# Split sums of squares and low parts on VectorE in a hybrid decoder layer

## The chip, the cores and the metric

The kernel runs on one core of one Trainium2 chip. The metric is the device time of one execution in microseconds (us): the median of the runs shown. A profile was taken of one execution.

The engines carry these names in the views: PE is TensorE's matmul and PEld its weight load, DVE is VectorE, ACT is ScalarE, POOL is GpSimd, and SP is SyncE, which here only issues DMAs. Each engine works through its own queue in order.

## The reference

One layer of a decoder is computed for a prompt of 2048 positions and 8 single-position samples, with a model width of 1024, 12 heads of 64 in three groups and a feed-forward width of 4096, all in float32:

```
shift1,scale1,g1,shift2,scale2,g2 = silu(c) @ w_ada + b_ada
h  = RMSNorm(x)*(1+scale1)+shift1
[u | q | k | v | a_pool | a_attn] = h @ w_in
x += g1 * ( sig(a_pool)*(PoolMix(u) @ w_pool_br) + sig(a_attn)*(DilatedAttn(q,k,v) @ w_attn_br) ) @ w_out
h2 = RMSNorm(x)*(1+scale2)+shift2
x += g2 * relu(h2 @ w_up)^2 @ w_down
```

PoolMix takes trailing means over 2, 4, 8 and 16 positions. DilatedAttn attends, in the three head groups, to 128 earlier positions at distances 1, 4 and 16. Before that each head of q and k is divided by the root mean square of its 64 elements and rotated (rope). The rotated keys and the values of the windows are returned too.

## The kernel before

**Number format.** Every large product is made of three products at TensorE's single rate in the type float32r: an operand is split into a high part (a cast to float32r on ACT) and a low part (the operand minus its high part), and high x high, high x low and low x high are summed. `mm3` issues them (24 products for one output tile of the width 1024). A product of plain float32 operands, as `small` issues it, is also used for small things, the sums of squares among them.

**Stages.** The positions are worked on in two phases (`ci` 0: the first 1024 positions and the 8 samples, `ci` 1: the other 1024), each in column groups of 512, 256 and 264 (phase 0) or 512 and 512 (phase 1). In order: the opening (`opening`: the first modulation blocks, the first norm and the first products); q, k and v of phase 0 (`qkv`), by head groups 2, 1, 0; gates, the rest of the modulation and the samples' attention; the pool branch of phase 0 and then of phase 1; q, k and v of phase 1 with the prompt's attention between its products; more gates; and from about 1375 us on, for each phase, the output projection (`project`), the second norm (`norm2`) and the feed-forward part (`up`, `down`), which fills the span from about 1530 us to the end.

**What sets the order.** TensorE's instructions run in the order in which the program writes them. The class `Order` keeps a planned time: each product adds its nominal nanoseconds, and generators that were spawned go on when the planned time has passed the amount that they yielded. The other engines' queues, SP's among them, are ordered by a scheduler when the kernel is built; `first()` gives the instructions in it a higher priority there. At run time every queue is in order, and an instruction that waits holds up those behind it.

**Weights.** `weights` (L213) hands out weights in the order of a plan and issues the load of the next one ahead. `load_w` (L178) loads 512 KB into one of three raw buffers, casts the high part on ACT (L183) and makes the low part on the engine that it was given (L184). `weights` always gives it POOL; the modulation weights `w_ada` use VectorE. A raw buffer can be loaded again when its low part is done.

**Modulated rows.** `modulated` (L317) is called by `make_h` (L356) for the first norm and by `norm2` (L1246) for the second, for each of the eight blocks k of 128 channels: a multiply on VectorE (L320), scale and shift on ACT (L321), high part on ACT (L326), low part on VectorE for even k and on POOL for odd k (L327).

**q and k.** For each of the 30 column groups of a q or k tile pair, `qk_out` (L388) evacuates two tiles on ACT, as values (`ab`, L390) and as squares (`qsq`, L391), and `after_qk` (L400) is spawned: it loads the rope table (L404, SP), adds the squares of the two halves on POOL (L405), makes the two sine products on POOL (L409, L411), the cosine products and sums on VectorE (L410, L412 to L414), and waits in the plan for `HS_AT` = 6500 ns. Then one float32 product with the matrix `hones` (1 where two rows belong to the same head) sums the squares per head and spreads the sum (L417), the root is taken on ACT (L419) and the reciprocal on VectorE (L420), both halves are scaled (L422), cast on ACT (L444), their low parts made on POOL (L445), and the four pieces are stored by SP (L450, L453, L456). The tile for these pieces (`ohl`) has one buffer; the table (`cs`) has two in phase 0 and one in phase 1. `hones` is a part of the packed constants, loaded first of all.

Of the kernel before, what the change touches and what calls it, by code (L numbers as in the profile page):

```python
# [16 lines left out]
P = 128  # L17
# [11 lines left out]
DEPTH = 1  # L29
HS_AT = 6500  # L30
ADA_GAP = 3600
# [20 lines left out]
PRIO = 400  # L52
CPACK = (("cT", (8, 9)), ("bada", (48,)), ("gn", (2, 8)), ("ident", (128,)), ("ones", (128,)), ("hones", (128,)),
         ("mask", (256,)), ("qkg", (2, 2)), ("psc", (4,)), ("icnt", (4, 16)), ("stT", (4, 8, 15)), ("fold", (9,)),
# [60 lines left out]
def emit(tc, I, O):  # L115
# [33 lines left out]
    def first():  # L149
        return tc.high_priority(offset=PRIO)  # L150
# [17 lines left out]
    def small(ps, w, x, ns=220.0):  # L168
        mm(ps, w, x, True, True, ns)
# [40 lines left out]
    issued = [0]  # L210
    depth = [DEPTH]

    def weights(*key):  # L213

        i = issued[0] - len(ready)
        assert plan[i] == key, (plan[i], key)
        while issued[0] < len(plan) and issued[0] <= i + depth[0]:
            k = plan[issued[0]]
            src = I[k[0]][k[1]] if len(k) == 2 else I[k[0]][k[1], :, k[2] * 1024:(k[2] + 1) * 1024]
            ready.append(load_w(src, G, *(extra if issued[0] == 3 else ())))  # L220
            issued[0] += 1
        return ready.pop(0)
# [4 lines left out]
    cv = {}  # L227
    off = 0
    for name, shape in CPACK:
# [7 lines left out]
        off += n  # L237
    cT, ident, ones, hones, mask = cv["cT"], cv["ident"], cv["ones"], cv["hones"], cv["mask"]
    bada, gn, qkg, icnt, stT = cv["bada"], cv["gn"], cv["qkg"], cv["icnt"], cv["stT"]
    epsc = cst.tile([P, 1], F32, name="epsc")  # L240
    V.memset(epsc, EPS)
# [74 lines left out]

    def modulated(hf, x, xr, rs, n, i, k, dst, c0, samp, eng):  # L317

        sh = (0 if i == 0 else 24) + k
        V.tensor_tensor(out=xr, in0=x, in1=rs[:, :n], op=ALU.mult)  # L320
        S.activation(out=hf[:, :n], in_=xr, func=AF.Identity, scale=sc[:, i, k, 0:1], bias=mod[:, sh, 0:1])  # L321
        if samp:
            sl = slice(n - NS, n)
            V.tensor_tensor(out=hf[:, sl], in0=xr[:, sl], in1=sc[:, i, k, 1:9], op=ALU.mult)
            V.tensor_tensor(out=hf[:, sl], in0=hf[:, sl], in1=mod[:, sh, 1:9], op=ALU.add)
        S.copy(out=dst[:, k, 0, c0:c0 + n], in_=hf[:, :n])  # L326
        eng.tensor_tensor(out=dst[:, k, 1, c0:c0 + n], in0=hf[:, :n], in1=dst[:, k, 0, c0:c0 + n].bitcast(F32), op=ALU.subtract)  # L327

# [9 lines left out]
    def hx(hb, nk, c0, n):  # L338
        return [(hb[:, k, 0, c0:c0 + n], hb[:, k, 1, c0:c0 + n]) for k in range(nk)]
# [16 lines left out]
    def make_h(ci, hi, xs, rs, hb, ks=range(KD)):  # L356
        c0, n, splits = HALVES[ci][hi]
        for k in ks:
            hf = npl.tile([P, 520], F32, tag="sq", bufs=3, name="hf")
            modulated(hf, xs[k], xs[k], rs, n, 0, k, hb, c0, ci == 0 and hi == 1, G if k % 2 else V)  # L360

# [31 lines left out]
    def qkv(ci, hb, done=None):  # L393
# [6 lines left out]
        def after_qk(g, qk, t0, n, ab, sq):  # L400
# [3 lines left out]
            SP.dma_start(out=cs[:, :, :n], in_=I["rope"][:, :, BASE[ci] - 1024 * ci + t0:BASE[ci] - 1024 * ci + t0 + n])  # L404
            G.tensor_tensor(out=sq[:, 0, :n], in0=sq[:, 0, :n], in1=sq[:, 1, :n], op=ALU.add)  # L405
            a, b, co, si = ab[:, 0, :n], ab[:, 1, :n], cs[:, 0, :n], cs[:, 1, :n]
            t = ap.tile([P, 2, 512], F32, tag="rt", bufs=1, name="rt")
            o = ap.tile([P, 2, 512], F32, tag="ro", bufs=2, name="ro")
            G.tensor_tensor(out=t[:, 0, :n], in0=b, in1=si, op=ALU.mult)  # L409
            V.tensor_tensor(out=o[:, 0, :n], in0=a, in1=co, op=ALU.mult)  # L410
            G.tensor_tensor(out=t[:, 1, :n], in0=a, in1=si, op=ALU.mult)  # L411
            V.tensor_tensor(out=o[:, 1, :n], in0=b, in1=co, op=ALU.mult)  # L412
# [3 lines left out]
            pst = stp.tile([P, 512], F32, tag="st", name="ps_hs")  # L416
            small(pst[:, :n], hones, sq[:, 0, :n], n / 0.6)  # L417
            rs = ap.tile([P, 512], F32, tag="qrs", bufs=2 - ci, name="qrs")
            S.activation(out=rs[:, :n], in_=pst[:, :n], func=AF.Sqrt, scale=1.0 / 64, bias=epsc)  # L419
            V.reciprocal(out=rs[:, :n], in_=rs[:, :n])  # L420
            for i in range(2):
                V.tensor_tensor(out=o[:, i, :n], in0=o[:, i, :n], in1=rs[:, :n], op=ALU.mult)  # L422
            ohl = ap.tile([P, 2048], F32R, tag="ohl", bufs=1, name="ohl")
            dst = (kst if qk else qst)[g]
# [323 lines left out]
    def opening():  # L748
# [10 lines left out]
        x1 = load_x0(op, 1)  # L759
        raws[3] = ada_load(op, 3)  # L760
        hxs = hx(h0, KD, 0, 512)

# [483 lines left out]
    def norm2(ci, hi, acc, hb, xa):  # L1246
        c0, n, splits = HALVES[ci][hi]
        yield 2500
        rs = rms_finish(tp, stp, acc, splits)
        for k in range(KD):  # L1250
            hg, hf = wtile("hg"), wtile("hf")
            modulated(hf, xa[k][:, c0:c0 + n], hg[:, :n], rs, n, 1, k, hb, 0, ci == 0 and hi == 1, G if k % 2 else V)

# [67 lines left out]
    for ci in range(2):  # L1321
# [15 lines left out]
        br = od.spawn(branches(ci, 1, hbs[1], GAP_B), 3000)  # L1337
        depth[0] = DEPTH_O
        acc = project(ci, 0, hbs[0], xa, load_xa)
        od.drain(br)  # L1340
# [140 lines left out]
```

## Time and profile before

| | |
|---|---|
| runs (us) | 3063.06, 3064.57, 3058.80 |
| median (us) | 3063.06 |
| profiled execution (us) | 3062.32 |
| its span, first to last instruction (us) | 3060.5 |
| mean granted TensorE clock, share of full speed | 0.98 |

The span is what the views divide up; the execution's own time lies 1.8 us above it. A group of instructions is given with its busy time, the mean of one in nanoseconds and the idle time of its engine just before it, with what ended that. A busy TensorE is not one at its peak, since the ends of its products are modelled and overlap.

### The profile page before, as it was taken

The numbers are of one execution on the slowest core, as the hardware profiler recorded it, in microseconds if no ns is written. First come the engines' busy times: TensorE is split into PE (matmuls) and PEld (weight loads), VectorE is DVE, ScalarE is ACT, GpSimd is POOL, SyncE is SP. The second block draws the span as 40 slices with busy tenths as digits, with TensorE's granted clock in tenths as the row PEclk, the third lists the DMA queues.
The fourth block names the chain that finished last, engine by engine and source line by source line (L and its number), as shares of the span: only waits on it lengthen the run. The fifth ranks groups of instructions, "written<-read, shape, count | busy, mean of one in ns | idle before, by whom it ended". The sixth has DMA issues, their size and how long they took to land.

```text
span 3060.5 us, 40917 instructions
## 1 busy us (share of the span) xinstructions
PE 2933.8 (96%) x16220; PEld 2510.3 (82%) x16220; DVE 1590.5 (52%) x2649; ACT 982.3 (32%) x1772; POOL 966.2 (32%) x510
## 2 busy tenths in 40 slices
PE   6899999999898799999999999999999999999999
PEld 3899788887787688878899999999877888888887
DVE  5556442541744534456865545555677554444444
ACT  5333342433554534433521221121235211111211
POOL 2665341433533312233532122122245312221221
PEclk7999999999999889999999999999999999999999
DMA  6544752335777779876321111111272211111111
GB/s 239 172 144 154 270 183 92 118 118 151 200 196 203 186 191 229 239 243 218 105 78 48 43 49 49 42 51 47 92 242 83 76 42 56 48 49 42 55 43 69
DMA packets 207599, 379.09 MB, mean 124 GB/s; under 512 B 47424, under 2 KB 103072, under 8 KB 206624
## 3 DMA queue, kind: packets, MB, share of 16 engines
q1 hardware_dynamic: 195888, 359.63, 38.6%
q10 hardware_dynamic: 11520, 16.85, 1.5%
q8 instruction: 128, 2.10, 0.3%
q14 instruction: 63, 0.52, 0.1%
HBM read 294.89 MB, written 81.75 MB: 123 GB/s over the span
## 4 chain that ended last, share of the span: by engine, by line
PE 76%; DMA 5%; DVE 5%; issue 4%; POOL 3%; ACT 2%; SPq 1%; ACTq 0%; DVEq 0%; POOLq 0%
PE ps_dn L153 23%; PE ps_up L153 22%; PE ps_g L153 10%; PE ps_v L153 4%; PE ps_qk L153 4%; PE ps_wo L153 3%; PE ps_u L153 3%; PE ps_o L153 1%; PE ps_pb L153 1%; POOL wh L184 1%; PE ps_s L153 1%; PE ps_ada L153 1%; DMA slab<-kst 1%; DMA cs<-in_rope 1%; PE ps_ab L153 1%
## 5 line engine op out<-in xcount | busy, mean ns | idle before, releaser
L184 POOL TENSOR_TENSOR wh<-wr,wh 128x1024 fp32r<-128x1024 f32 (+1 forms) x274 | 649.3, 2377 | 1637.9 <-ACT wh L183 1620.7
L153 PE MATMUL ps_dn<-rt,wh 128*128 128x512 f32 (+2 forms) x3840 | 727.0, 350 | 5.3 <-POOL wh L184 3.3
L153 PEld LDWEIGHTS ps_dn<-rt,wh 128*128 128x128 f32 x3840 | 619.6, 188 | 108.2 <-POOL wh L184 4.2
L183 ACT CAST wh<-wr 128x1024 fp32r<-128x1024 f32 (+1 forms) x306 | 309.4, 1023 | 737.9 <-issue 564.0
L1306 DVE SCALAR_TENSOR_TENSOR xa<-ps_dn,mod,xa 128x512 f32<-128x512 f32 (+1 forms) x640 | 405.2, 642 | 202.1 <-PE ps_dn L153 195.9
L153 PE MATMUL ps_g<-h,wh 128*128 128x512 f32 (+2 forms) x1920 | 389.6, 354 | 0.4 <-POOL wh L184 0.4
L153 PE MATMUL ps_up<-hb,wh 128*128 128x264 f32 (+2 forms) x2304 | 371.7, 319 | 0.0
L153 PE MATMUL ps_up<-ha,wh 128*128 128x512 f32 x1536 | 367.3, 395 | 0.0
L153 PEld LDWEIGHTS ps_up<-hb,wh 128*128 128x128 f32 x2304 | 332.3, 188 | 36.1
L153 PEld LDWEIGHTS ps_g<-h,wh 128*128 128x128 f32 x1920 | 307.2, 190 | 48.5 <-POOL wh L184 1.0
L153 PEld LDWEIGHTS ps_up<-ha,wh 128*128 128x128 f32 x1536 | 286.6, 188 | 66.3 <-issue 0.5
L153 PE MATMUL ps_qk<-h,wh 128*128 128x512 f32 (+2 forms) x1440 | 301.4, 362 | 14.2 <-POOL wh L184 4.9
L1290 DVE TENSOR_TENSOR r<-r 128x512 f32<-128x512 f32 (+2 forms) x160 | 99.3, 621 | 389.2 <-ACT r L1289 389.1
L153 PEld LDWEIGHTS ps_qk<-h,wh 128*128 128x128 f32 x1440 | 233.6, 193 | 58.5 <-POOL h L327 6.3
L1292 DVE TENSOR_TENSOR rt<-r,rt 128x512 fp32r<-128x512 f32 (+2 forms) x160 | 218.0, 1362 | 81.7 <-ACT rt L1291 81.6
L1289 ACT ACTIVATE r<-ps_up 128x512 f32<-128x512 f32 (+2 forms) x160 | 82.1, 513 | 416.8 <-PE ps_up L153 416.8
L153 PE MATMUL ps_v<-wh,h 128*128 128x256 f32 (+1 forms) x1224 | 171.6, 297 | 25.4 <-ACT wh L183 19.3
L153 PEld LDWEIGHTS ps_v<-wh,h 128*128 128x128 f32 (+1 forms) x1224 | 157.8, 195 | 30.5 <-ACT wh L183 19.7
L945 ACT ACTIVATE pe<-pe,ost 128x128 f32<-128x128 f32 (+1 forms) x192 | 87.1, 454 | 142.5 <-DVE ost L943 139.5
L943 DVE CUSTOM_DVE_ANT_0 pe<-ps_s,cp 128x128 f32<-128x128 f32 (+1 forms) x192 | 61.5, 358 | 118.2 <-PE ps_s L153 118.0
L1291 ACT CAST rt<-r 128x512 fp32r<-128x512 f32 (+2 forms) x160 | 85.7, 536 | 66.4 <-DVE r L1290 66.4
L445 POOL TENSOR_TENSOR ohl<-ro,ohl 128x256 fp32r<-128x256 f32 (+1 forms) x66 | 76.1, 1175 | 92.4 <-ACT ohl L444 81.8
(182 smaller groups left out, 2981.7 us busy)
## 6 DMA issues: line engine op xcount, KB each, us to landing
wr<-in_w_up SPq DMA_DIRECT2D x72, 512.0 KB
wr<-in_w_down SPq DMA_DIRECT2D x68, 512.0 KB
wr<-in_w_in SPq DMA_DIRECT2D x64, 512.0 KB
wr<-in_w_ada SPq DMA_DIRECT2D x48, 512.0 KB
slab<-kst SPq DMA_DIRECT2D x40, 512.0 KB
wr<-in_w_out SPq DMA_DIRECT2D x32, 512.0 KB
cs<-in_rope SPq DMA_DIRECT2D x18, 512.0 KB
qst<-ohl SPq DMA_DIRECT2D x9, 1024.0 KB
```

The source lines that it names most:

```text
L153: PE.matmul(ps, w, x, start=start, stop=stop)
L183: S.copy(out=wt[:, 0, :n], in_=raw[:, :n])
L184: eng.tensor_tensor(out=wt[:, 1, :n], in0=raw[:, :n], in1=wt[:, 0, :n].bitcast(F32), op=ALU.subtract)
L445: G.tensor_tensor(out=pl, in0=pi, in1=ph.bitcast(F32), op=ALU.subtract)
L943: V.tensor_tensor_reduce(out=pe[:, off:off + nk], in0=ps[:, off:off + nk], in1=mask[:, mo:mo + nk], scale=-0.125, scalar=3.0e38, op0=ALU.a ...
L945: S.activation(out=pe[:, off:off + nk], in_=pe[:, off:off + nk], func=AF.Exp, scale=-1.0, bias=o[:, 64:65], accum_out=o[:, 65:66])
L1289: S.activation(out=r1[:, :l], in_=ps[:, :l], func=AF.Relu)
L1290: V.tensor_tensor(out=r1[:, :l], in0=r1[:, :l], in1=r1[:, :l], op=ALU.mult)
L1291: S.copy(out=rt[:, 0, a:a + l], in_=r1[:, :l])
L1292: V.tensor_tensor(out=rt[:, 1, a:a + l], in0=r1[:, :l], in1=rt[:, 0, a:a + l].bitcast(F32), op=ALU.subtract)
L1306: V.scalar_tensor_tensor(out=x[:, c0 + a:c0 + a + lp], in0=ps[:, :lp], scalar=mod[:, 40 + m, 0:1], in1=x[:, c0 + a:c0 + a + lp], op0=ALU.m ...
```

## The change

The low parts of the modulated rows are all made on VectorE. `weights` gives `load_w` the engine `weng[0]`, which is VectorE until the output projection of phase 0 begins and POOL from there on. The two sine products of the rope go to VectorE. The sum of squares per head is split into a high part (ACT) and a low part (VectorE), and two single-rate products with `hones` take the place of the float32 one; they are planned 9000 ns after the column group instead of 6500. The two parts live in the buffers of the gates' tile `th` (two buffers; a group of 512 or 264 columns takes both, one of 256 takes one). `hones` becomes a float32r constant of its own, loaded in the opening through a raw weight buffer and cast on ACT. `ohl` has two buffers in phase 0.

```diff
-HS_AT = 6500
+HS_AT = 9000
...
-CPACK = (("cT", (8, 9)), ("bada", (48,)), ("gn", (2, 8)), ("ident", (128,)), ("ones", (128,)), ("hones", (128,)),
+CPACK = (("cT", (8, 9)), ("bada", (48,)), ("gn", (2, 8)), ("ident", (128,)), ("ones", (128,)), 
...
+    weng = [V]
...
-            ready.append(load_w(src, G, *(extra if issued[0] == 3 else ())))
+            ready.append(load_w(src, weng[0], *(extra if issued[0] == 3 else ())))
...
+    hones = cst.tile([P, P], F32R, name="hones")
...
-    def modulated(hf, x, xr, rs, n, i, k, dst, c0, samp, eng):
+    def modulated(hf, x, xr, rs, n, i, k, dst, c0, samp):
...
-        eng.tensor_tensor(out=dst[:, k, 1, c0:c0 + n], in0=hf[:, :n], in1=dst[:, k, 0, c0:c0 + n].bitcast(F32), op=ALU.subtract)
+        V.tensor_tensor(out=dst[:, k, 1, c0:c0 + n], in0=hf[:, :n], in1=dst[:, k, 0, c0:c0 + n].bitcast(F32), op=ALU.subtract)
...
             G.tensor_tensor(out=sq[:, 0, :n], in0=sq[:, 0, :n], in1=sq[:, 1, :n], op=ALU.add)
+
+            m = 1 if n > 256 else 2
+            hl = [gtp.tile([P, m, 512 // m], F32R, tag="th", bufs=2, name="sqhl") for _ in range(2 // m)]
+            sh, sl = (hl[0][:, 0, :n], hl[-1][:, m - 1, :n])
+            with first():
+                S.copy(out=sh, in_=sq[:, 0, :n])
+                V.tensor_tensor(out=sl, in0=sq[:, 0, :n], in1=sh.bitcast(F32), op=ALU.subtract)
...
-            G.tensor_tensor(out=t[:, 0, :n], in0=b, in1=si, op=ALU.mult)
+            V.tensor_tensor(out=t[:, 0, :n], in0=b, in1=si, op=ALU.mult)
             V.tensor_tensor(out=o[:, 0, :n], in0=a, in1=co, op=ALU.mult)
-            G.tensor_tensor(out=t[:, 1, :n], in0=a, in1=si, op=ALU.mult)
+            V.tensor_tensor(out=t[:, 1, :n], in0=a, in1=si, op=ALU.mult)
...
-            small(pst[:, :n], hones, sq[:, 0, :n], n / 0.6)
+            mm(pst[:, :n], hones, sh, True, False, max(107.0, n / 2.4 + 2.5))
+            mm(pst[:, :n], hones, sl, False, True, max(107.0, n / 2.4 + 2.5))
...
-            ohl = ap.tile([P, 2048], F32R, tag="ohl", bufs=1, name="ohl")
+            ohl = ap.tile([P, 2048], F32R, tag="ohl", bufs=2 - ci, name="ohl")
...
         raws[3] = ada_load(op, 3)
+        raw = rawp.tile([P, 1024], F32, tag="wr", name="wr")
+        SP.dma_start(out=raw[:, :P], in_=I["hones"])
+        S.copy(out=hones, in_=raw[:, :P])
...
         depth[0] = DEPTH_O
+        weng[0] = G
         acc = project(ci, 0, hbs[0], xa, load_xa)
```

The calls of `modulated` lose their last argument (`G if k % 2 else V`).

## Rows read from the trace of the kernel before

**Rows 1.** The page's first part: busy time, share of the span, instructions of each engine.

```profile
PE 2933.8 (96%) x16220; PEld 2510.3 (82%) x16220; DVE 1590.5 (52%) x2649; ACT 982.3 (32%) x1772; POOL 966.2 (32%) x510
```

**Rows 2.** What TensorE's products waited for: us in total, times, longest.

```profile
PE ps_v L153 <- ACT wh L183: 19.3, 2, 16.2
...
PE ps_hs L153 <- POOL qsq L405: 5.1, 3, 2.5
PE ps_qk L153 <- POOL wh L184: 4.9, 2, 3.2
...
PE ps_qk L153 <- POOL h L327: 4.6, 4, 3.9
PE ps_v L153 <- POOL wh L184: 4.6, 3, 2.8
```

**Rows 3.** Groups of TensorE's products by form: busy us, mean ns | idle before.

```profile
L153 PE MATMUL ps_up<-ha,wh 128*128 128x512 f32 x1536 | 367.3, 395 | 0.0
...
L153 PE MATMUL ps_up<-hb,wh 128*128 128x256 f32 x768 | 95.5, 280 | 0.0
...
L153 PE MATMUL ps_hs<-qsq,cp 128*128 128x512 f32 x36 | 18.9, 607 | 2.6 <-POOL qsq L405 2.6
...
L153 PE MATMUL ps_hs<-qsq,cp 128*128 128x256 f32 x12 | 3.6, 379 | 0.0
```

**Rows 4.** TensorE in order of time, 159 to 167 us: start, us, merged products.

```profile
159.82 1.02 PE L153 MATMUL ps_hs<-qsq,cp 128*128 128x512 f32 x2
160.28 5.64 PE L153 MATMUL ps_qk<-h,wh 128*128 128x264 f32 x39
165.76 0.59 PE L153 MATMUL ps_hs<-qsq,cp 128*128 128x256 f32 x2
```

**Rows 5.** Line 184, the weights' low parts: ns min/median/max, first and last start.

```profile
L184 POOL TENSOR_TENSOR wh<-wr,wh x274: 1278/2399/3405, 36.5 to 3025.0; 128x1024 fp32r<-128x1024 f32 x134, 128x512 fp32r<-128x512 f32 x3
L184 DVE TENSOR_TENSOR wh<-wr,wh x32: 1205/1226/3339, 295.0 to 488.6; 128x1024 fp32r<-128x1024 f32 x32
```

**Rows 6.** Line 327, the modulated rows' low parts of the first norm, on VectorE.

```profile
L327 DVE TENSOR_TENSOR h<-hf,h x16: 680/701/2481, 32.9 to 634.3; 128x512 fp32r<-128x512 f32 x12, 128x520 fp32r<-128x520 f32 x4
```

**Rows 7.** All engines in order of time, 81 to 88 us.

```profile
81.66 0.68 ACT L326 CAST h<-hf 128x520 fp32r<-128x520 f32 x1
...
85.15 1.72 POOL L327 TENSOR_TENSOR h<-hf,h 128x520 fp32r<-128x520 f32 x1
...
86.93 1.39 PE L153 MATMUL ps_qk<-h,wh 128*128 128x256 f32 x6 [3.88 <-POOL h L327]
```

**Rows 8.** Busy us in two stretches; then 142 to 192, lines 445 and 405 alone.

```profile
142.00:192.00 50.00, 49.57 (x311) 44.04 (x310) 29.37 (x28) 23.16 (x41) 36.26 (x28) 1.00 0.52 158
1480.00:1530.00 50.00, 45.50 (x235) 37.60 (x235) 41.69 (x58) 25.20 (x37) 23.74 (x12) 1.00 0.36 116
...
142.00:192.00 50.00, 8.31 (x8) 1.00 0.52 158
...
142.00:192.00 50.00, 5.69 (x5) 1.00 0.52 158
```

The columns of the first two are PE, PEld, DVE, ACT and POOL, then the granted clock, the DMA engines' share and GB/s; the last two have POOL alone.

**Rows 9.** Groups by form from 142 to 192 us, VectorE and POOL.

```profile
L184 POOL TENSOR_TENSOR wh<-wr,wh 128x1024 fp32r<-128x1024 f32 x5 | 12.0, 2401 | 0.4 <-ACT wh L183 0.4
...
L420 DVE RECIPROCAL qrs<-qrs 128x512 f32<-128x512 f32 x2 | 6.7, 3354 | 0.5 <-ACT qrs L419 0.5
...
L413 DVE TENSOR_TENSOR ro<-ro,rt 128x512 f32<-128x512 f32 x2 | 3.1, 1560 | 1.2 <-POOL rt L409 1.2
...
L414 DVE TENSOR_TENSOR ro<-ro,rt 128x512 f32<-128x512 f32 x2 | 1.4, 680 | 0.0
```

**Rows 10.** All queues in order of time, 1050 to 1069 us.

```profile
1060.50 0.57 SPq L456 DMA_DIRECT2D kst<-ohl  x1
...
1061.12 0.62 SPq L180 DMA_DIRECT2D wr<-in_w_v  x1
...
1068.82 0.58 PE L153 MATMUL ps_v<-wh,h 128*128 128x256 f32 x1 [16.22 <-ACT wh L183]
```

More of the change, by code (lines that the diff above doesn't have):

```diff
@@ L237, in emit @@
         off += n
-    cT, ident, ones, hones, mask = cv["cT"], cv["ident"], cv["ones"], cv["hones"], cv["mask"]
+    cT, ident, ones, mask = cv["cT"], cv["ident"], cv["ones"], cv["mask"]
     bada, gn, qkg, icnt, stT = cv["bada"], cv["gn"], cv["qkg"], cv["icnt"], cv["stT"]
+    hones = cst.tile([P, P], F32R, name="hones")
     epsc = cst.tile([P, 1], F32, name="epsc")
@@ L359, in make_h @@
             hf = npl.tile([P, 520], F32, tag="sq", bufs=3, name="hf")
-            modulated(hf, xs[k], xs[k], rs, n, 0, k, hb, c0, ci == 0 and hi == 1, G if k % 2 else V)
+            modulated(hf, xs[k], xs[k], rs, n, 0, k, hb, c0, ci == 0 and hi == 1)
     def subs(ci):
@@ L1251, in norm2 @@
             hg, hf = wtile("hg"), wtile("hf")
-            modulated(hf, xa[k][:, c0:c0 + n], hg[:, :n], rs, n, 1, k, hb, 0, ci == 0 and hi == 1, G if k % 2 else V)
+            modulated(hf, xa[k][:, c0:c0 + n], hg[:, :n], rs, n, 1, k, hb, 0, ci == 0 and hi == 1)
     def project(ci, hi, hb, xa, load_xa=None):
```

## The prediction

> **What bounds the kernel now.** I read the page's busy line first. TensorE is busy 96% of the span and VectorE and GpSimd 52% and 32% [rows 1], so the program is one long line of TensorE work in a fixed order, and time can be won in two ways only: fewer TensorE microseconds, or fewer waits of TensorE. The second view was therefore the list of what TensorE waits for [rows 2]. It is short. Of the waits that this change can reach, one group is 19.3 us, the v product waiting for a weight's high part, with 16.2 us in a single wait. The others go back to GpSimd (POOL): 5.1 us for the sums of squares, 4.9 us for weights of the q and k products, 4.6 us for the normalised rows, 4.6 us for weights of the v products. That makes 38.5 us. The third view was TensorE's groups, for what one product costs [rows 3, 4], then those of the two elementwise engines, by line, in order of time and by stretch [rows 5 to 9], and last the stretch with the longest wait [rows 10]. After about 1530 us only the 16 low parts of odd rows in the second norm change, so the argument is about the first half.
>
> The profiled execution took 3062.3 us around a span of 3060.5; the median of the runs is 3063.1, 0.7 us more, and I let the forecast stand for both. About 0.2%, 6 us, is what a measurement of this kernel can tell from no change.
>
> **The change, part by part.**
>
> *A. Sums of squares as two single-rate products.* There are 30 such products, 18 of 512 columns and 12 of about half. Now each is two records: 18.9 us for 18 wide ones, 1.05 us each, and 3.6 us for six narrow ones, 0.60 us each; those of 264 columns are alike [rows 3]. A single-rate product costs 367.3/1536 = 0.239 us at 512 columns and 95.5/768 = 0.124 us at 256 [rows 3], so two cost 0.48 and 0.25. Upper end: 18 x 0.57 + 12 x 0.35 = 14.5 us. A record may overlap its neighbours, so the lower end is taken from starts: from 159.82 to 165.76 TensorE issued one wide product and 39 products of about half width [rows 4]; 39 x 0.129 (the 256 price scaled to 264) leaves 0.91 us for the wide one, a gain of 0.43, and half of it for a narrow one: 18 x 0.43 + 12 x 0.21 = 10.3 us. I take **-12**.
>
> *B. Weights and normalised rows in the opening.* The low part of a weight takes 2.40 us on POOL and 1.23 us on VectorE (medians) [rows 5]; that of a row takes 0.70 us on VectorE [rows 6] and 1.72 us on POOL where it matters [rows 7]. The longest wait for a weight is 3.2 us [rows 2], in the opening. At least the difference of 1.17 goes, at most all 3.2; I take 2.2. The longest for a row is 3.9: ACT ended the last high part at 82.34, but POOL began the low part only at 85.15, because its queue held rope and squares ahead of it, and TensorE resumed at 86.93 [rows 7]. On VectorE 1.0 (the difference) to 3.9 is gained; I take 3, since the sines that hold up VectorE at that point come from POOL today. The remaining 1.7 and 0.7 us of these two groups I put at 0.8. Together **-6**, ends 2.2 and 9.5 (1.17 + 1.0, and all of both groups).
>
> *C. The later product.* It is issued 2.5 us later by the plan (9000 instead of 6500), and there are two new steps ahead of it, a cast on ACT of about 0.7 us [rows 7] and a low part on VectorE of about 0.7 us [rows 6]. So 1.1 us more slack than now, and of the 5.1 us of waits I let **-3** go; ends 0 and 5.1. Behind it everything that follows the product is later too: the root, the reciprocal, the high and low parts and the store that stands in SP's queue.
>
> *D. Weights of the v products.* Three waits, 4.6 us; each low part is 1.17 us shorter. I take **-2.4**, ends 0 and 4.6.
>
> *E. The wait of 16.2 us.* SP issues in order. The store of k (1060.50) stands in front of the weight load (1061.12), and TensorE starts again at 1068.82 [rows 10]. The store ends a chain of rope operations on both engines. VectorE operations of 512 columns take 0.68 us alone and 1.56 beside POOL [rows 9]; with the sines moved, four of them shorten by about 0.9 us. I take **-4**. Upper end: all 19.3 go, as the order of the queue is made anew; lower end: +2.5, when the store is only later by the moved product.
>
> *F. What VectorE takes over.* The stretch from 142 to 192 is one group's q and k products: 2 wide and 4 narrow. VectorE is busy 29.4 of 50 us, POOL 36.3 [rows 8]. Added: sines 4 x 0.68 + 8 x 0.4, low parts of sums 2 x 0.68 + 4 x 0.4, five weights (POOL's count there, [rows 9]) x 1.23; together 15.1 us (0.4 is an estimate for half of 0.68). TensorE needs 2.2 us less, so VectorE is busy 44.5 of 47.8, and the cover is thin. A low part of a sum may find a reciprocal of 3.35 us running [rows 9]; with half of it, one operation in front and its own time it is 3.1 us against the 2.5 us of C, 0.6 us for 18 wide products, about 10 us at worst and nothing at best. I take **+4**.
>
> *G. The second norm.* Four low parts per half, 2.8 us, come to VectorE where it is busy 41.7 of 50 us and TensorE idles 4.5 [rows 8]. POOL gets free for the weights that TensorE waits for there. I take 0, ends +5.6 (two such exposed places) and -2.
>
> *The rest at nothing.* The some 50 weights of the gates, u and pool products (VectorE has 48% of the span free [rows 1], and a weight is asked for one ahead, which covers a low part that is late by up to a column group of 24 x 0.239 = 5.7 us [rows 3]; a queue longer than that costs the excess); the separate load of the 128x128 matrix, one DMA on SP in the opening and a small cast on ACT, which takes one of three raw buffers at a time when the next weight is not yet needed, while the packed constants shrink by the same bytes; the second buffer for the stored parts, which only shortens waits of ACT. If the opening's cover is gone, the DMA costs its own landing of some us once.
>
> Sum: -12 - 6 - 3 - 2.4 - 4 + 4 = -23.4, and 3062.3 - 23.4 = **3039 us**.
>
> **The rivals.**
>
> 1. *Slower: VectorE becomes the bound of the q and k stretches.* Place: the three such stretches of the first phase. POOL keeps 8.3 + 5.7 = 14.0 us of low parts and sums in the stretch [rows 8]. If each of these microseconds stops VectorE, it needs 44.5 + 14.0 = 58.5 of 47.8 us, 10.7 too many, and TensorE waits for the low parts of the sums: 3 x 10.7 = 32 us against A + B + D = 20.4, so 3062.3 - 20.4 + 32 = 3074 us. It decides from 6.8 us per stretch. For it: the pairs 0.68 and 1.56 us [rows 9]. Against it: today's 29.4 us already hold the collisions with 36.3 us of POOL, of which 22 go. Chance 0.12. The Trainium skill, SBUF — State Buffer, "Who interferes with whom", has VectorE operations with two SBUF inputs and GpSimd reads exclude one another for a whole instruction; the trace agrees in kind (0.68 and 1.56 us). By that rule the 58.5 of this rival is the load to reckon with, where the sum above goes by today's mixture.
>
> 2. *Only A stays.* The waits of B to E are short and spread; a wait removed lets TensorE run into the next one (DMA in the opening, slabs later). Then 3062 - 12 = 3050 us. Chance 0.2.
>
> 3. *The long wait goes too.* If VectorE's own order starts the rope earlier, the store no longer stands in front of the weight load: A 12, B 8, C 5, D 4.6, 16.2: 3062.3 - 45.8 = 3016 us. Chance 0.15.
>
> 4. *No change.* SP's order is made anew for every kernel, and a new wait as long as the 16.2 can arise elsewhere: without E the sum is -19.4, and with such a wait -3.2: 3059 us. Chance 0.11.
>
> **How the numbers follow.** The forecast has 0.42. All upper ends at once give 3062.3 - 55 = 3007, all lower ends (10.3 + 2.2 - 2.5 - 10 - 5.6 = -5.6) 3068. The range from 3012 to 3066 holds the forecast's own cases, rivals 2 to 4, and leaves out rival 1 and some of the ends. Faster by over 0.2%: 0.42 + 0.2 + 0.15 = 0.77; within 0.2%: 0.11; slower: 0.12.
>
> **What would show it.** A: ps_hs in 60 records at about 0.24 and 0.12 us. B: the waits of TensorE for POOL's weights and rows gone from its list, the opening shorter by some 6 us. C: waits for the product's low part under 2 us in all. F: VectorE near 45 us in the first q and k stretches, without TensorE idle. E: whether the single longest wait is above or below 12 us. I am wrong if VectorE's low parts head TensorE's list, if the opening is not shorter, or if a new SP order brings a wait of over 16 us.

## The result and the profile after

The changed kernel takes **3034.0 us** (median of six runs, 3030.0 to 3042.0) against 3063.1 us of the kernel before in the same session (median of five runs; a sixth, of 8137 us, is left out). The ratio is 0.9912, with a 95% interval of 0.9897 to 0.9927. The forecast was 3039. The profiled execution took 3030.4 us around a span of 3028.6. The number came out nearly as forecast, but the runs below show that the steps behind it did not.

The page's first part, which answers to [rows 1]:

```profile
PE 2917.0 (96%) x16220; PEld 2503.8 (83%) x16220; DVE 1671.0 (55%) x2858; ACT 998.9 (33%) x1803; POOL 639.0 (21%) x331
```

POOL lost 327 us of work, VectorE gained only 81, the 30 new low parts of the sums included. What TensorE waits for (us, times, longest), against [rows 2]:

```profile
PE ps_t L172 <- ACT pe L958: 14.3, 8, 3.6
PE ps_v L153 <- ACT wh L183: 11.9, 1, 11.9
...
PE ps_qk L153 <- ACT h L328: 3.2, 1, 3.2
PE ps_qk L153 <- DVE wh L184: 2.9, 2, 2.5
...
PE ps_v L153 <- DVE wh L184: 1.5, 1, 1.5
```

The waits of the q, k, v and per-head products for POOL are gone. One long wait for a v weight is still there. A new line, the attention's transposes behind ScalarE, heads the list with 14.3 us; without the split (experiment 3) it is 7.8 us. The per-head products by form (busy us, mean ns | idle before), against [rows 3]:

```profile
L153 PE MATMUL ps_hs<-sqhl,hones 128*128 128x512 f32 x36 | 11.9, 412 | 0.0
L153 PE MATMUL ps_hs<-sqhl,hones 128*128 128x264 f32 x12 | 2.8, 301 | 0.7 <-ACT sqhl L413 0.5
L153 PE MATMUL ps_hs<-sqhl,hones 128*128 128x256 f32 x12 | 2.4, 279 | 0.0
```

A wide product costs 11.9/18 = 0.66 us busy, not 1.05 as before.

To see where the 31.9 us of span went, I cut each trace at the first TensorE product of a kind. This table, worked out from the traces, also holds kernels of the experiments (us). Some products of the attention lie on the other side of a cut from kernel to kernel, so third v and the gates behind it are best read as a sum.

```
stretch                        before  after  no_split  no_split_6500  c_alone  split_alone   best
start to first v                110.7  105.3     101.3           98.8    111.2        110.9  102.2
q/k/v of first phase, rest      180.8  173.2     175.4          175.7    179.3        183.9  172.3
gates of first phase            213.0  209.3     213.1          211.4    215.8        220.1  210.9
u, pools, norm of second phase  239.5  238.5     238.1          238.4    240.6        240.7  239.2
second phase, first two groups  224.7  219.4     217.7          217.6    231.4        234.9  219.3
third q/k                        82.3   78.8      80.8           79.7     79.3         80.2   78.4
third v                          72.1   66.3      53.2           57.2     52.3         76.9   58.2
gates of second phase           256.0  262.7     267.9          264.5    273.4        264.3  263.8
output projection               108.3  107.2     107.8          107.6    107.4        107.2  108.4
rest                           1573.1 1568.0    1567.7         1567.8   1572.7       1572.0 1568.4
span                           3060.5 3028.6    3023.2         3018.6   3063.5       3091.1 3021.1
```

Before to after, the gain is in the opening (5.4 us), the rest of the first q/k/v part (7.6), the first gates (3.7), the second phase's first two groups (5.3), third q/k (3.5), third v (5.8) and the second norm and what follows (5.1); the second gates give 6.7 us back.

### The profile page after: what moved, and what is told of

It is laid out like the page before. It is cut to its first block, busy times and chain, and to the rows that moved or that the text cites. A ratio compares the mean times of both kernels' runs of the same rounds, so it can differ in the third digit from the quotient of the medians.

```text
span 3028.6 us, 40868 instructions
## 1 busy us (share of the span) xinstructions
PE 2917.0 (96%) x16220; PEld 2503.8 (83%) x16220; DVE 1671.0 (55%) x2858; ACT 998.9 (33%) x1803; POOL 639.0 (21%) x331
## 4 chain that ended last, share of the span: by engine, by line
PE 54%; DMA 4%; issue 3%; POOL 3%; DVE 2%; ACT 0%; SPq 0%; POOLq 0%; ACTq 0%; DVEq 0%
PE ps_up L153 24%; PE ps_dn L153 23%; PE ps_g L153 4%; POOL wh L184 3%; DMA wr<-in_w_out 1%; PE ps_o L153 1%; DMA slab<-kst 1%; PE ps_s L153 1%; DMA t<-t1d 1%; DMA wr<-in_w_attn_br 1%; PE ps_t L172 1%; PE ps_v L153 0%; PE ps_ab L153 0%; ACT wh L183 0%; DVE t L1201 0%
## 5 line engine op out<-in xcount | busy, mean ns | idle before, releaser
L184 POOL TENSOR_TENSOR wh<-wr,wh 128x1024 fp32r<-128x1024 f32 (+1 forms) x187 | 436.2, 2342 | 1295.3 <-ACT wh L183 1280.6
L153 PEld LDWEIGHTS ps_up<-ha,wh 128*128 128x128 f32 x1536 | 286.6, 188 | 66.3 <-issue 0.5
L184 DVE TENSOR_TENSOR wh<-wr,wh 128x1024 fp32r<-128x1024 f32 x119 | 157.2, 1328 | 140.5 <-ACT wh L183 133.7
L153 PE MATMUL ps_v<-wh,h 128*128 128x256 f32 (+1 forms) x1224 | 163.2, 287 | 14.5 <-ACT wh L183 11.9
L153 PEld LDWEIGHTS ps_v<-wh,h 128*128 128x128 f32 (+1 forms) x1224 | 150.7, 187 | 17.4 <-ACT wh L183 12.1
L407 POOL TENSOR_TENSOR qsq<-qsq 128x512 f32<-128x512 f32 (+2 forms) x30 | 36.8, 1226 | 384.7 <-ACT qsq L393 381.7
```

The costliest lines, as they stand in the source:

```text
L153: PE.matmul(ps, w, x, start=start, stop=stop)
L184: eng.tensor_tensor(out=wt[:, 1, :n], in0=raw[:, :n], in1=wt[:, 0, :n].bitcast(F32), op=ALU.subtract)
```

## The experiments

Twelve kernels, each timed against the kernel before on the same chip. That one's medians were 3062.1 to 3065.5 us, so the ratios are what is to be compared; the changed kernel's is 0.9912, and 0.0010 of a ratio is 3.1 us. Where a difference from the changed kernel is given by the medians, the one by the ratios stands beside it; two ratios together leave it uncertain by some 6 us.

**1. The split alone** (the kernel before with A and C; the cast, the low part and the separate load of the matrix are included and left out of this cut):

```
-            small(pst[:, :n], hones, sq[:, 0, :n], n / 0.6)
+            mm(pst[:, :n], hones, sh, True, False, ...)
+            mm(pst[:, :n], hones, sl, False, True, ...)
...
-HS_AT = 6500
+HS_AT = 9000
```

> The kernel before plus parts A and C alone (the split per-head sum as two products, and the later product); all of POOL's work stays on POOL. Theory 1, the parts add up: the per-head products fall from 26.2 to about 17 us of busy time and their waits for POOL's sums vanish with the later product, so 9 to 14 us less than before: 3050 to 3055. Rival, the split needs an unburdened POOL: the cast on ScalarE stands first in its queue and waits for POOL's sum, which comes late behind POOL's own weights and sines; ScalarE's wait for the summed squares grows from 21.0 us (the changed kernel) to over 60 us, and the time is the before's or worse, 3060 to 3075.

3091.9 us, ratio 1.0095 (1.0082 to 1.0108): 29 us **slower** than before. The direction is the rival's, and worse than its 3075. ScalarE's wait for the sum came to 45.5 us, between the two figures. VectorE's and ScalarE's waits around the split, then SP's queue and the product behind it:

```profile
DVE sqhl L413 <- ACT sqhl L412: 70.0, 14, 36.7
...
ACT sqhl L412 <- POOL qsq L406: 45.5, 24, 5.8
```

```profile
1079.63 0.57 SPq L405 DMA_DIRECT2D cs<-in_rope  x1
...
1084.65 0.57 SPq L465 DMA_DIRECT2D kst<-ohl  x1
1085.27 0.62 SPq L180 DMA_DIRECT2D wr<-in_w_v  x1
```

```profile
PE ps_v L153 <- ACT wh L183: 26.7, 2, 21.5
```

The long wait of [rows 10], 16.2 us there, is 21.5 us here, again with the v weight's load behind the store of k.

**2. The later product alone** (C):

```
-HS_AT = 6500
+HS_AT = 9000
```

> The kernel before with the later product alone (part C). Theory 1: with POOL loaded, the later product takes away waits for POOL's sums, 5.1 us in all, and costs at most as much behind it: 3058 to 3065, so that the 29 us which split and later product cost together are the split's. Rival, it is the later product that costs them, since root, high and low parts and the stores in SP's queue come later: 3075 or more.

3068.8 us, ratio 1.0018 (1.0008 to 1.0027): no gain but a small loss, a little above the first theory's range and far below the rival's. So of the 29 us some 23 (3091.9 against 3068.8) are those of the split with its separate load. The table shows a second thing: the long wait is gone here (third v 52.3 against 72.1 us), and the gates take 17.4 us more. Together they are 325.7 against 328.1: a 16 us wait removed, 2.4 us won. Of the 17.4 us, 5 are busy time, since products moved across the cut (1346 records instead of 1323). The other 12 are idle time (22.5 against 10.3 us). Among the waits in the gates' stretch are those for the gates' weights, of which the kernel before has 0.4 us there:

```profile
PE ps_g L153 <- ACT wh L183: 5.4, 2, 3.2
...
PE ps_g L153 <- POOL wh L184: 5.0, 5, 1.7
```

**3. The changed kernel without the split** (float32 product, matrix packed, C kept; the cast, the low part and the load go too and are left out of this cut):

```
-            mm(pst[:, :n], hones, sh, True, False, ...)
-            mm(pst[:, :n], hones, sl, False, True, ...)
+            small(pst[:, :n], hones, sq[:, 0, :n], n / 0.6)
```

> The changed kernel with the one float32 product over the sum instead of the split (later product kept). Theory 1: only A is lost, 9 to 12 us: 3043 to 3046, and the 30 wide and narrow products take 26 us of busy time again. Rival, the split's cast and low part, which go first in their queues, cost as much as the product saves (the long wait of 11.9 us for a w_v tile, the 21.0 us of ScalarE behind POOL's sum): without them 3026 to 3036, and the long wait at 1037.9 us is under 5 us.

3024.3 us, ratio 0.9873 (0.9859 to 0.9886): 9.7 us **faster** than the changed kernel by the medians, 12 by the ratios. The rival was right, by more than it said, and the long wait is gone from the list (that line has 1.1 us left). One q/k stretch in the first phase, by the view of busy time in stretches (columns as [rows 8]), in the changed kernel and here:

```profile
132.80:179.50 46.70, 46.70 (x299) 42.30 (x298) 33.26 (x46) 22.34 (x41) 12.72 (x11) 1.00 0.58 177
```

```profile
127.90:175.70 47.80, 47.80 (x298) 42.55 (x297) 31.68 (x43) 20.26 (x36) 12.49 (x11) 1.00 0.51 156
```

TensorE is busy throughout in both, so here the split does what it should: 1.2 us a stretch (46.6 against 47.8 between the starts of its first and the next stretch's products), and 0.4 us (26.2 against 26.6) in the v stretch behind it. What it loses lies elsewhere.

**4. The matrix back among the packed constants**, the split kept:

```
-        SP.dma_start(out=raw[:, :P], in_=I["hones"])
-        S.copy(out=hones, in_=raw[:, :P])
+        S.copy(out=hones, in_=cv["hones"])
```

> The changed kernel with the 128x128 matrix back among the packed constants, and only cast into its own tile. Theory 1: its separate load took one of three raw buffers at 30.55 us and moved the next two weight loads from 30.55 to 36.48 us; without it the wait of 2.49 us for the second weight's low part falls under 1 us and the stretch to the first v product from 70.4 to 67 to 69 us: 3029 to 3033. Rival, the load costs nothing in the time of the whole: 3033 to 3036, and the stretch is 70 to 71 us.

3029.1 us, ratio 0.9894 (0.9878 to 0.9910); the stretch from the first q/k product to the first v product is 67.7 instead of 70.4 us. That is as the theory had it, though the interval overlaps the changed kernel's. SP's queue and TensorE in the changed kernel, then here:

```profile
30.55 0.33 SPq L772 DMA_DIRECT2D wr<-in_hones  x1
36.48 0.80 SPq L180 DMA_DIRECT2D wr<-in_w_in  x2
```

```profile
52.52 4.64 PE L153 MATMUL ps_qk<-h,wh 128*128 128x512 f32 x10 [2.49 <-DVE wh L184]
```

```profile
30.21 1.69 SPq L180 DMA_DIRECT2D wr<-in_w_in  x2
```

```profile
50.57 2.78 PE L153 MATMUL ps_qk<-h,wh 128*128 128x512 f32 x7 [0.75 <-DVE wh L184]
```

The small load takes one of three raw buffers, the next weights' load moves from 30.2 to 36.5 us, and the second weight is late by 2.49 instead of 0.75 us. So about half of experiment 3's gain is this load (4.9 of 9.7 us by the medians, 5.5 of 12 by the ratios). The rest is the split, and by the traces it lies in the second phase: its third v stretch is 66.5 us here and 53.2 without the split, of which the gates and the projection behind it give 7 back.

**5. The split in program order**, not ahead in its queues:

```
-            with first():
-                S.copy(out=sh, in_=sq[:, 0, :n])
-                V.tensor_tensor(out=sl, ...)
+            S.copy(out=sh, in_=sq[:, 0, :n])
+            V.tensor_tensor(out=sl, ...)
```

> The changed kernel with the split's cast and low part in their queues in the order of the program, not ahead of the rope products. Theory 1, the long wait comes from that low part standing ahead of the previous group's rope: the wait of 11.9 us for a w_v tile falls under 4 us and the time to 3022 to 3029. Rival, the split costs its time wherever it stands (its tiles, ScalarE's cast behind POOL's sum): the wait stays above 8 us, 3031 to 3040.

3038.4 us, ratio 0.9918 (0.9905 to 0.9931). No difference from the changed kernel, and the long wait was 17.0 us, both as the rival had them. VectorE in order of time:

```profile
1029.98 0.69 DVE L413 TENSOR_TENSOR sqhl<-qsq,sqhl 128x512 fp32r<-128x512 f32 x1 [2.35 <-ACT sqhl L412]
1035.86 0.69 DVE L417 TENSOR_TENSOR rt<-ab,cs 128x512 f32<-128x512 f32 x1 [5.18 <-DMA cs<-in_rope]
```

The low part stood ahead of the previous group's rope all the same, and the rope then waited for its table, which SP had issued at 1021.73. So at this place the edit did not bring about the order that my theory was about. The theory's numbers failed, and whether that order would help is not shown.

**6. The second phase's tables through POOL's queue.** The changed kernel's queues ahead of the long wait (several engines, in order of time):

```profile
1025.87 1.26 POOL L407 TENSOR_TENSOR qsq<-qsq 128x512 f32<-128x512 f32 x1 [17.07 <-ACT qsq L393]
1027.17 0.62 ACT L413 CAST sqhl<-qsq 128x512 fp32r<-128x512 f32 x1 [1.37 <-POOL qsq L407]
1027.82 0.69 DVE L414 TENSOR_TENSOR sqhl<-qsq,sqhl 128x512 fp32r<-128x512 f32 x1 [2.35 <-ACT sqhl L413]
1028.43 0.68 DVE L418 TENSOR_TENSOR rt<-ab,cs 128x512 f32<-128x512 f32 x1
...
1030.95 0.57 SPq L406 DMA_DIRECT2D cs<-in_rope  x1
...
1031.57 0.59 SPq L180 DMA_DIRECT2D wr<-in_w_v  x1
...
1036.02 0.57 SPq L466 DMA_DIRECT2D kst<-ohl  x1
...
1037.88 0.79 PE L153 MATMUL ps_v<-wh,h 128*128 128x256 f32 x2 [11.90 <-ACT wh L183]
```

Sum, cast and low part of one column group stand ahead of the rope of the group before; that rope holds the table's only buffer, SP waits with the next table, and behind it stands the v weight.

```
-            SP.dma_start(out=cs[:, :, :n], in_=I["rope"]...)
+            if ci == 0:
+                SP.dma_start(out=cs[:, :, :n], in_=I["rope"]...)
             G.tensor_tensor(out=sq[:, 0, :n], ...)
+            if ci:
+                G.dma_start(out=cs[:, :, :n], in_=I["rope"]...)
```

> The changed kernel with the second phase's rope tables loaded through POOL's queue, behind the sum of squares, instead of SP's. Theory 1: the long wait for a w_v tile is SP standing at a table load that waits for the previous group's rope (1030.95 us) with the w_v load behind it (1031.57 us) and 7.6 us after the last load ahead of it was issued: with the table out of the way the wait falls from 11.9 us to under 6, and the time to 3024 to 3030. Rival, the table is one of several: SP then stands at the store of k, or the weight waits for its raw buffer, the wait stays above 9 us and the time is 3031 to 3040.

3049.4 us, ratio 0.9961 (0.9946 to 0.9976). The wait did vanish (third v 55.2 instead of 66.3 us), so what stood ahead of the v weight was the table; the time got worse by 15 us, which neither theory had. Third q/k went from 78.8 to 93.4 us and the gates from 262.7 to 271.0:

```profile
1022.49 0.72 POOL L410 DMA_DIRECT2D cs<-in_rope  x1 [0.85 <-DVE ro L424]
...
1036.41 0.69 DVE L422 TENSOR_TENSOR ro<-ab,cs 128x512 f32<-128x512 f32 x1 [9.40 <-DMA cs<-in_rope]
...
1037.62 0.42 DVE L979 COPY ost<-ps_o 128x256 f32<-128x256 f32 x1
...
1038.19 1.94 PE L153 MATMUL ps_o<-vt,px 128*128 128x64 f32 x8 [4.91 <-DVE ost L979]
```

The table was used 13.9 us after its issue. VectorE stood 9.4 us at the rope, an attention copy stood behind that, and TensorE waited 4.9 us for the copy. So this run doesn't tell what the long wait alone was worth.

**7 to 9. Each kind of work back on POOL**, the split kept: weights, sines, odd rows.

```
-    weng = [V]
+    weng = [G]
```

> The changed kernel with the weights' low parts on POOL throughout (part D and the weight terms of part B undone). Theory 1: the first weights cost 2.8 us at the opening and the v-product weights 2.4 us, and POOL's sums come later behind 2.40 us low parts: 3036 to 3042. Rival, the weights were never what bounded (TensorE works ahead of them and the gain is the split and the rows): within 2 us of the changed kernel, 3029 to 3034.

```
-            V.tensor_tensor(out=t[:, 0, :n], in0=b, in1=si, op=ALU.mult)
+            G.tensor_tensor(out=t[:, 0, :n], in0=b, in1=si, op=ALU.mult)
...
-            V.tensor_tensor(out=t[:, 1, :n], in0=a, in1=si, op=ALU.mult)
+            G.tensor_tensor(out=t[:, 1, :n], in0=a, in1=si, op=ALU.mult)
```

> The changed kernel with the two sine products of each group on POOL again. Theory 1: VectorE was not the bound (34 to 35 of 47 to 48 us busy), POOL is late with the sums, the splits and their casts wait behind the sine products: 3036 to 3046. Rival, taking over the sines costs what part F priced (4 us), and VectorE is freed: 3026 to 3030.

```
-            modulated(hf, xs[k], xs[k], rs, n, 0, k, hb, c0, ...)
+            modulated(hf, xs[k], xs[k], rs, n, 0, k, hb, c0, ..., G if k % 2 else V)
...
```

> The changed kernel with the odd modulated rows' low parts on POOL again, at the opening and in the second norm. Theory 1: the two stretches from the first up products to the end (741.0 and 827.0 us in the changed kernel, 743.3 and 829.8 before, 743.2 and 828.8 with the split alone) go back to about 743 and 829 us, and the opening from the first q/k product to the first v product goes from 70.4 back to 73 to 75 us: 3040 to 3044. Rival, rows on VectorE are worth only the opening (part G at nothing): 3036 to 3039 with 741 and 827 unchanged.

Weights 3055.7 us, ratio 0.9982 (0.9973 to 0.9991); sines 3052.3, 0.9968 (0.9955 to 0.9980); rows 3047.9, 0.9950 (0.9937 to 0.9963). Undone singly, they cost 21.7, 18.3 and 13.9 us by the medians and 21, 17 and 12 by the ratios, each more than any of my theories gave it.

*Weights* lose in the first v stretch (32.3 against 27.5 us), the first gates (216.2 against 209.3) and the second phase, and nothing in the opening (105.4 against 105.3). The first v stretch shows how (several engines, in order of time):

```profile
109.49 3.42 DVE L432 TENSOR_TENSOR ro<-ro,qrs 128x256 f32<-128x256 f32 x2
110.11 2.53 POOL L184 TENSOR_TENSOR wh<-wr,wh 128x1024 fp32r<-128x1024 f32 x1
112.84 0.94 DVE L414 TENSOR_TENSOR sqhl<-qsq,sqhl 128x256 fp32r<-128x256 f32 x1
113.83 0.46 PE L153 MATMUL ps_hs<-sqhl,hones 128*128 128x256 f32 x1 [4.24 <-DVE sqhl L414]
```

Two scalings on VectorE, 0.42 us each elsewhere, take 3.42 beside the weight's low part on POOL. The low part of the sum stands behind them in VectorE's queue, and the product waits 4.24 us for it.

*Sines* lose in the opening (108.0 against 105.3), the second phase's first q/k stretch (71.9 against 64.9) and third v (74.0 against 66.3), where the long wait is 21.4 instead of 11.9 us.

*Rows* lose 4.0 us in the opening's q/k stretch, 5.8 in the second phase's first norm (172.7 against 166.9 for its stretch), and 4.3 in the second norm. In the first norm of the second phase the u product waits 2.8 us for a weight's high part, a wait that neither the changed kernel nor the kernel before has there (their stretches are 166.9 and 167.9). The second norm's part shows in two views of the same stretch of its first half, changed kernel first; the second half adds as much (829.1 against 827.0 us):

```profile
1460.60:2201.60 741.00, 737.73 (x4662) 666.58 (x4661) 424.84 (x774) 172.74 (x292) 172.96 (x74) 1.00 0.19 64
```

```profile
1468.90:2212.10 743.20, 738.15 (x4662) 666.42 (x4661) 424.72 (x770) 172.88 (x292) 179.20 (x78) 1.00 0.20 64
```

**10. No split, product at 6500** (experiment 3 without C):

```
-HS_AT = 9000
+HS_AT = 6500
```

> The kernel without the split and with the product due at 6500 again instead of 9000 (part C undone as well). Theory 1: POOL has the sums ready early now, so the later product brings nothing without the split: within 2 us of the kernel without the split, 3022 to 3027. Rival, the later product is worth what part C priced (3 us) or more: 3027 to 3032, with TensorE waiting for POOL's sums by 2 us or more in the trace.

3022.0 us, ratio 0.9866 (0.9852 to 0.9879), with experiment 3 inside the interval: C brings nothing that can be measured. This is also the kernel before with the moves to VectorE and the second store buffer alone: **41 us**.

The second buffer was not undone by itself. It takes away ScalarE's waits for the stores. They stand in the kernel before and are gone here:

```profile
ACT ohl L444 <- DMA qst<-ohl: 29.3, 7, 5.8
ACT ohl L444 <- DMA kst<-ohl: 27.1, 5, 8.5
```

All twelve of them lie between 112 and 286 us, where the table's second row gains 5.1 us from the kernel before to this one (180.8 against 175.7), with the moved weights among the causes. So the buffer's direct part looks small; what it does to later stretches is not shown.

**11. The split in the last two groups of the first phase alone**, float32 elsewhere:

```
+            split = ci == 0 and g < 2
```

> The changed kernel with the split only in the last two groups of the first phase, one float32 product elsewhere. Theory 1, the split pays where TensorE waits for nothing (46.6 against 47.8 us for the second and third q/k stretch, 26.2 against 26.6 us for the v stretch behind each) and costs at the opening and in the second phase: 3.2 us less than the kernel without the split, 3020 to 3022. Rival, what is saved there is given back later in the first phase: 3023 to 3026.

3021.8 us, ratio 0.9864 (0.9851 to 0.9877), within the theory's range, its difference from experiment 3 inside the intervals. The opening's q/k stretch has no split and still takes 71.1 us, since it keeps the separate load: experiment 4 from the other side.

**12. What stood, together** (experiment 11, matrix packed, unsplit products due at 6500):

```
+            split = ci == 0 and g < 2
-            yield HS_AT
+            yield HS_AT if split else 6500
-        SP.dma_start(out=raw[:, :P], in_=I["hones"])
-        S.copy(out=hones, in_=raw[:, :P])
+        S.copy(out=hones, in_=cv["hones"])
```

> What the runs left standing, together: the moves to VectorE, the split in the last two groups of the first phase alone (due at 9000), one float32 product elsewhere (due at 6500), the 128x128 matrix among the packed constants. Theory 1, the parts add up: the kernel without the split at 6500 had 3022.0 us, and two groups save 1.6 us each: 3017 to 3021. Rival, the order of the queues in the second phase comes out anew and takes it back: 3022 to 3030, with the stretch from the first q/k product of the second phase to the first up product over 725 us (722 in the kernel without the split at 6500).

**3016.4 us**, ratio 0.9846 (0.9833 to 0.9859): below both kernels, and the lowest of the study, though its interval overlaps that of experiment 10. Its profiled execution was the longest of its five (3022.9), so its column in the table is on the high side. From the second phase's first q/k product to the first up product it has 728.1 us against 726.6 in experiment 10 (the 722 and with it the mark of 725 in the expectation were a misreading of mine), so the queues there gave nothing back to speak of.

## Why the prediction was right, and where it was not

The forecast rested on A for half of its gain, on 11 us of POOL's waits (B, C, D), on 4 us of the long wait (E) and on a loss of 4 us for what VectorE takes over. The moves to VectorE with the second store buffer gave 41 us, and the split, its load and the later product took 12 of them back by the medians (3034.0 against 3022.0), 14 by the ratios. The errors had opposite signs, and that the sum hit was luck.

- **A, -12: failed.** Its step "two cost 0.48 and 0.25" was nearly right where TensorE is the bound: 1.6 us a group there (1.2 and 0.4), which would be 9.6 for six, against a lower end of 10.3. What the step left out is the chain that the split puts between the squares and the product: POOL's sum, a cast on ScalarE and a low part on VectorE, at the head of in-order queues that also carry the scaling and the rope. With POOL loaded this cost 23 us net, the separate load included (experiments 1, 2). With POOL relieved and the load undone it was about 5 by the medians and 6 by the ratios, with intervals that overlap (3, 4).
- **"The rest at nothing", the separate load: failed.** I gave it some us if the cover was gone, and it was gone: about 5 us of the whole by the medians, 2.7 of them in the opening's q/k stretch. They come less from its own landing than from the raw buffer that it takes from the next weights (experiment 4).
- **B, -6, D, -2.4, and the gates' weights at nothing: right in sign, too small.** Without the split, its load and the later product the opening is 11.9 us shorter (98.8 against 110.7), above B's upper end of 9.5. In the changed kernel, undoing the rows costs 4.0 us in the opening, near B's 3; undoing the weights costs nothing there, where the separate load holds up the second weight anyway (experiment 4), and 21.7 us elsewhere. Two terms are missing. A low part on POOL stretches the VectorE operation beside it and so delays what stands behind that in VectorE's queue (the 4.24 us of experiment 7); and POOL's sums come later when its queue is fuller, though by ScalarE's wait for them this is seen with the sines alone (40.9 us with the sines on POOL, 18.4 with the weights, 20.3 with the rows, 21.0 in the changed kernel). And a wait is paid twice. TensorE in the second v stretch of the second phase, in the kernel before and in that of experiment 10:

```profile
917.90:968.70 50.80, 40.40 (x289) 38.76 (x288) 27.42 (x56) 23.44 (x47) 20.98 (x12) 0.87 0.76 207
```

```profile
922.53 0.50 PE L153 MATMUL ps_v<-wh,h 128*128 128x256 f32 x2 [3.07 <-ACT wh L183]
925.80 4.42 PE L153 MATMUL ps_v<-wh,h 128*128 128x256 f32 x19 [2.77 <-POOL wh L184]
```

```profile
925.80:930.22 4.42, 4.42 (x20) 4.42 (x21) 4.22 (x9) 3.82 (x4) 2.60 (x2) 0.50 0.13 53
```

```profile
900.50:941.80 41.30, 35.43 (x288) 33.49 (x287) 26.26 (x56) 23.46 (x47) 7.81 (x5) 1.00 0.89 243
```

```profile
905.01 2.52 PE L153 MATMUL ps_v<-wh,h 128*128 128x256 f32 x19 [0.76 <-DVE wh L184]
```

  Of 9.5 us, 4.5 are idle time (10.4 against 5.9). The other 5.0 are busy time of the same products at a granted clock of 0.87 instead of 1.00: nineteen products took 4.42 us behind waits of 3.07 and 2.77, and 2.52 us where the waits ahead of them were 1.67 and 0.76: 0.233 and 0.133 each. In the slow 4.42 us the granted clock was 0.50, the lower of its two levels (1.2 and 2.4 GHz). I had priced waits at their length.
- **C, -3: failed.** Alone it made no gain (1.0008 to 1.0027); undone without the split it changed nothing measurable. With the split it was not undone.
- **E, -4: right in size for the wait, wrong in its way and as a term.** The wait went from 16.2 to 11.9 us, just under my mark of 12. But I had the store of k leave sooner, and in the changed kernel it stands behind the weight load (1036.02 against 1031.57), which is rival 3's condition; the rest of the wait is the table's (experiment 6). With the sines on POOL beside the split the store stands in front and the wait is 21 us (experiments 1 and 8), so the sines' move is worth more to this wait than the 4 us, by a change of order that I had put into rival 3. That the size agreed is luck. Nor is a shorter wait there time won at its length: where it is gone, third v and the gates together keep 2.4 of the 19.8 us by which third v gets shorter (experiment 2), or 7.9 of 13.1 (experiment 3 against the changed kernel). Rival 3, which took the whole 16.2 for a gain, had the same fault.
- **F, +4: wrong sign.** Putting the sines back costs 18.3 us. The step "VectorE is busy 44.5 of 47.8" counted the added work and kept the old durations; measured are 33.26 of 46.7 us. The pair of [rows 9], 0.68 and 1.56 us, was the hint: with less work on POOL more of the wide operations take the short time. In this stretch five of eight kinds of wide two-input operations on VectorE take 0.66 to 0.69 us on average and three 1.02 to 1.23; in the kernel before one of five takes 0.68, the others 1.23 to 1.69. Two of the changed kernel's kinds, one of either sort:

```profile
L422 DVE TENSOR_TENSOR ro<-ro,rt 128x512 f32<-128x512 f32 x2 | 2.0, 1015 | 0.0
...
L420 DVE TENSOR_TENSOR rt<-ab,cs 128x512 f32<-128x512 f32 x2 | 1.3, 674 | 0.0
```

- **G, 0: failed on the good side**, a gain of 4.3 us (experiment 9) with 2 as its end. No term held the second phase's first norm: undoing the rows costs 5.8 us there, though from the kernel before to the changed one that stretch gained only 1.0.
- **Rival 1, the VectorE bound, is refuted** by experiment 3's row of the changed kernel: TensorE is busy 46.70 of 46.70 us there. The Trainium skill, SBUF — State Buffer, "Who interferes with whom", has VectorE operations with two SBUF inputs and GpSimd reads exclude one another. In the split-alone kernel, a rope product of 0.69 us took 1.75 beside POOL's of 1.77:

```profile
1076.12 0.69 DVE L418 TENSOR_TENSOR ro<-ab,cs 128x512 f32<-128x512 f32 x1 [1.41 <-DMA cs<-in_rope]
1076.17 1.77 POOL L417 TENSOR_TENSOR rt<-ab,cs 128x512 f32<-128x512 f32 x1 [2.83 <-DMA cs<-in_rope]
1076.73 1.75 DVE L420 TENSOR_TENSOR ro<-ab,cs 128x512 f32<-128x512 f32 x1
```

  So the trace agrees with the rule at this place; I had weighed it only as a danger, while taking work off POOL is what it speaks for.
- **What would show it**: the waits for POOL left the list, the opening is 5.4 us shorter, the product waits 0.5 us in all (the group of 264 columns above). The records of the product took 0.41 and 0.28 to 0.30 us, not 0.24 and 0.12, and VectorE was busy 33 us, not near 45. None of these views could have shown that A lost time; only undoing it did.

Rival 2, by which only A stays, came out the other way round: nearly everything but A stays.

The three undoings are not to be held against the 41 us, which is what the moves bring without the split. With the split and its load in both kernels, from experiment 1 to the changed kernel, the moves and the second store buffer bring 57.9 us by the medians and 56 by the ratios; the three singly come to 53.9 and 50. So the split makes a burdened POOL dearer: 41 us without it, 58 with it.

What stays open: where the whole of the 21.7 us of the weights lies beyond the wait shown in the first v stretch, and what the second store buffer gives. The three were not undone singly without the split. And the queues are ordered anew for every kernel, so an undoing also makes waits that have nothing to do with its own work, like the u product's 2.8 us.

## What to carry to other kernels

When work moves off an engine that shares memory access with its neighbour, price the neighbour's old work anew: here VectorE ended with 209 instructions more for only 81 us, and in the q/k stretch it was busy 33 us where 44.5 had been reckoned. A cheaper operation that needs two new steps ahead of it in in-order queues is to be costed by what stands behind those steps, and one undone part on the chip tells more than a total that came out as forecast. A single long wait is not a reserve of its own length: see what the stretch behind it does when it is gone. And price an undoing against a kernel that has the same other parts.

## Not expected of the hardware

A rope table of the same size took 4.6 us from issue to first use in the changed kernel (1030.95 to the rope at 1035.55), 13.9 us through POOL's queue among the attention's stores, and 14.1 us through SP's queue in experiment 5 (1021.73 to the rope at 1035.86). So POOL's queue alone does not explain it; what does is not shown. And the granted clock made idle time dear twice over: 0.233 us a product at 0.50 behind waits of 3 us, instead of 0.133 at 1.00.
